# Deeper lead of logits and softmax in an attention stage, and LayerNorm rows fetched in pairs

## The chip, the cores and the metric

The kernel is one program on one core of a Trainium2 chip. The metric is device time in microseconds (us) of one execution. The core has five engines that run side by side, each through its own list of instructions and in the order of that list: TensorE (PE, matrix products), VectorE (DVE), ScalarE (ACT), GpSimd (POOL) and SyncE (SP, which here only issues DMA transfers). ACT and POOL issue DMA transfers too.

## The reference, cut to what matters

One decoder block over 1024 tokens of width 1024, in float32. A projection gives queries, keys and values, the input of a convolution, and merge gates. The attention has 8 heads in 2 groups and three branches (compressed, selected, window); the selection takes 16 of 16 blocks, so the selected branch is causal attention over all keys. Beside it a convolution of width 31 is followed by a LayerNorm over 512 channels and a product with `w_conv_out`. The two paths are gated, summed and multiplied by `w_out`; a gated feed-forward part and a gated embedding term (`p @ w_ple`) follow.

```python
o = gates[0] * o_c + gates[1] * o_s + gates[2] * o_w
y_a = o @ w_o_nsa[i]
c = jax.nn.silu(layernorm(c, conv_ln_g[i], conv_ln_b[i]))
y_b = c @ w_conv_out[i] + b_conv_out[i]
h = h + (ga * y_a + gb * y_b) @ w_out[i]
...
h = h + gate * (p[i] @ w_ple[i])
```

## The kernel before

Every product keeps float32 precision by splitting both operands into a high and a low part (ACT writes the high part, DVE or POOL subtracts it from the original) and adding three products. Weights come through `w_fetch`, which keeps two raw tiles in flight on SP's queue, and `w_split`, which splits the oldest of them (ACT L102, then L105 on DVE, or on POOL during attention); `w_get` hands out split weights in the order of one list, and splits on the spot when none is ready.

The two calls of `attention(g, ...)` are the stage that the change touches. The work of a group is 32 *units*: 8 blocks of 128 queries (`i`), 2 pairs of heads (`hp`), 2 branch kinds (`br` 1: compressed and selected keys, 2: window). A unit runs through three steps. `qk_steps` makes logits: PE multiplies queries with keys into a PSUM bank, and DVE moves them, masked and with their row maximum, into the unit's tile S in SBUF (L677, L689, L692). `soft_steps` is the softmax: DVE reduces the maximum (`ngm`, L712), ACT takes the exponent (L717), DVE makes the factor `r` (L721, L722), POOL multiplies blocks of S by it (L702, `norm`). `av_steps` makes the products with the values: PE transposes a pair of blocks of S (L758), ACT and DVE split them into P (L160, L161), and PE multiplies P by v. The last of these comes three steps late (`LAG = 3`), so that the split has time.

S has two tiles for each kind of branch:

```python
un.S = at([128, 2, T], "S1", bufs=2)
...
un.S = at([128, 2, 640], "S2", bufs=2)
```

`attention` goes over the units in order, and `weave` merges lists of steps by position: the products of unit n, the logits of unit n+2 in the first tenth, the softmax of unit n+1 in the first half, and filler steps that give PE work. A tile framework then simulates the program and fixes the order of each engine's instructions: a step that is written first has priority, but one that the simulation finds ready may be put ahead of it. On the chip that order is kept.

The filler of `attention(0)` is merge-gate chunks (`chunk_fill`, products of `u` with weights). The filler of `attention(1)` is, in this order: two gate chunks (the last one is chunk 31); `swap`, which closes the pool of `u`, opens the pool `cx` in its place and reads four tiles of 512 KB back on POOL's queue (L918); eight LayerNorm rows, of which `ln_b0` reads one from DRAM (`y_d`) on SP's queue and `ln_b1` transposes it on PE (L193) and splits it into `c2`; then `yb_fill` (y0 to y7, products of `c2` with `w_conv_out`) and `pw_fill` (p0, p1, p2, the embedding term; p3 is made elsewhere). Gate results, LayerNorm rows, and the tiles of `yb_fill` and `pw_fill` share three buffers of 4 KB per partition (tag "t").

The diff touches the list of weights (`late`), `attention`, `ln_b0`, `ln_b1` and the list `fill1`:

Of the kernel before, what the change touches and what calls it, by code (L numbers as in the profile page):

```python
# [34 lines left out]
def tile_hybrid_block(ctx: ExitStack, tc: tile.TileContext, a: dict, out: bass.AP):  # L35
    nc = tc.nc
# [26 lines left out]
    def weave(*lists):  # L63

        items = []
        for li, (l, lo, hi) in enumerate(lists):
            for j, f in enumerate(l):
                items.append((lo + (hi - lo) * (j + 0.5) / len(l), li, f))
        for _, _, f in sorted(items, key=lambda x: x[:2]):
            f()  # L70
# [17 lines left out]
    def w_fetch():  # L88
        while order and len(raws) < AHEAD:
            key, src, n, pl, th, tl = order.pop(0)  # L90
            raw = wp.tile([128, n], F32, tag="wr", name=nm("wr"))
            nc.sync.dma_start(raw, src)
            raws.append((key, raw, n, pl, th, tl))

    def w_split():

        w_fetch()
        if raws and raws[0][3] in pools:
            key, raw, n, pl, th, tl = raws.pop(0)
            hi = pools[pl].tile([128, n], F32R, tag=th, name=nm("wh"))  # L100
            lo = pools[pl].tile([128, n], F32R, tag=tl, name=nm("wl"))
            nc.scalar.activation(hi, raw, AF.Copy)  # L102
            for c0 in range(0, n, 512):
                cs = slice(c0, min(c0 + 512, n))
                lo_eng[0].tensor_tensor(lo[:, cs], raw[:, cs], hi[:, cs], op=ALU.subtract)  # L105
            raw_of[key] = raw
            made.append((key, (hi, lo)))
# [24 lines left out]
    for c in [0, 1] + gate_chunks[NDENSE:NDENSE + NFILL] + [2, 3] + gate_chunks[NDENSE + NFILL:]:  # L132
        add_z(c)
    EARLY, NE = (3,), 4
    late = ["y0", "y1", "p0", "y2", "p1", "y3", "y4", "p2", "y5", "y6", "p3", "y7"]
    late = [f for f in late if f[0] == "y" or int(f[1]) not in EARLY]
    held = None
    for f in late:
# [78 lines left out]
    y_d = dp.tile([8, 128, 512], F32, name="y_d")  # L217
# [395 lines left out]
    at = Pool("at", 6)  # L613
# [37 lines left out]
    def qk_steps(un):  # L651

        i, g = un.i, un.g
        KK = KS[g] if un.br == 1 else KW[g]
        th, t0 = i // 4, 128 * (i % 4)

        def step(h, si):
            if h == 0 and si == 0:
                un.mx = as_([128, 2, 8], "mx")
                if un.br == 1:  # L660
                    un.S = at([128, 2, T], "S1", bufs=2)
                    if un.hp == 0:
                        cbank[i] = (at([128, 4, 64], "cs", bufs=2), as_([128, 4], "cmx"))
                else:
                    un.S = at([128, 2, 640], "S2", bufs=2)
            S = un.S[:, h]
            q = Q[th][2 * g + un.hp][:, h, t0:t0 + 128]
            s, e = un.segs[si]
            ps = tt_()
            mm(ps[:, 0:e - s], q, KK[0][:, un.k0 + s:un.k0 + e], True, False)  # L670
            mm(ps[:, 0:e - s], q, KK[1][:, un.k0 + s:un.k0 + e], False, True)
            o = 0
            if un.nc and si == 0:
                o = un.nc
                C, cmx = cbank[i]
                hd = 2 * un.hp + h
                nc.vector.tensor_tensor_reduce(out=C[:, hd], in0=ps[:, 0:64], in1=cm[:, i], scale=0.125,  # L677
                                               scalar=-3e38, op0=ALU.add, op1=ALU.max,
                                               accum_out=cmx[:, hd:hd + 1])
            n = e - s - o  # L680
            d = slice(s + o - un.nc, e - un.nc)
            mxo = un.mx[:, h, si:si + 1]
            mask = None
            if si == un.nseg - 1:
                mask = dm[:, 512 - n:512]
            elif un.br == 2 and i >= 4 and si == 0:
                mask = em[:, 0:n]
            if mask is not None:
                nc.vector.tensor_tensor_reduce(out=S[:, d], in0=ps[:, o:e - s], in1=mask, scale=0.125,  # L689
                                               scalar=-3e38, op0=ALU.add, op1=ALU.max, accum_out=mxo)  # L690
            else:
                nc.vector.tensor_scalar(S[:, d], ps[:, o:e - s], 0.125, -3e38, op0=ALU.mult, op1=ALU.max,  # L692
                                        accum_out=mxo)

        return [(lambda h=h, si=si: step(h, si)) for h in range(2) for si in range(un.nseg)]
# [8 lines left out]
    def soft_steps(un):  # L704

        i, g = un.i, un.g
        nk = un.n - un.nc
        gi = un.br * 8 + g * 4 + un.hp * 2

        def s_max():  # L710
            un.ngm = as_([128, 2], "ngm")
            nc.vector.tensor_reduce(un.ngm, un.mx[:, :, 0:un.nseg], axis=AX.X, op=ALU.max, negate=True)  # L712
            un.sm = as_([128, 2], "sm")
            un.r = as_([128, 2], "r")

        def s_exp(h):
            nc.scalar.activation(un.S[:, h, 0:nk], un.S[:, h, 0:nk], AF.Exp, bias=un.ngm[:, h:h + 1],  # L717
                                 accum_out=un.sm[:, h:h + 1])

        def s_r():  # L720
            nc.vector.reciprocal(un.r, un.sm)  # L721
            nc.vector.tensor_mul(un.r, un.r, gts[:, i, gi:gi + 2])  # L722

        def c_sub():
            C, cmx = cbank[i]
            nc.gpsimd.tensor_tensor(C, C, cmx.unsqueeze(2).to_broadcast([128, 4, 64]), op=ALU.subtract)
            nc.scalar.activation(C, C, AF.Exp)

        def c_norm():
            C, cmx = cbank[i]  # L730
            csm, rc = as_([128, 4], "csm"), as_([128, 4], "rc")
            nc.vector.tensor_reduce(csm, C, axis=AX.X, op=ALU.add)
            nc.vector.reciprocal(rc, csm)
            nc.vector.tensor_mul(rc, rc, gts[:, i, g * 4:g * 4 + 4])
            nc.gpsimd.tensor_tensor(C, C, rc.unsqueeze(2).to_broadcast([128, 4, 64]), op=ALU.mult)

        st = [s_max, lambda: s_exp(0), lambda: s_exp(1), s_r]
        if un.cmp:
            st.insert(1, c_sub)
            st.insert(3, c_norm)  # L740
        st += [lambda b=b: norm(un, b) for b in range(min(NAHEAD, (un.nb + 1) // 2))]
        return st
# [79 lines left out]

    WA, WB, WC = 0.5, 3, 0.1

    def attention(g, pre, fill, tail=()):

        units = [Unit(i, g, hp, br) for i in range(8) for hp in range(2) for br in (1, 2)]
        nu = len(units)
        est = [units[n].av + (units[n + 2].qk if n + 2 < nu else 0) for n in range(nu)]
        total = sum(t for t, _ in fill)  # L830
        want = [max(WA * e, WB - e) + WC for e in est]
        scale = total / sum(want)
        weave((qk_steps(units[0]) + soft_steps(units[0]) + qk_steps(units[1]), 0, 1), (pre, 0, 1))
        due, done = 0.0, 0.0
        for n, un in enumerate(units):
            lists = [(av_steps(un), 0, 1)]
            if n + 2 < nu:
                lists.append((qk_steps(units[n + 2]), 0, 0.1))
            if n + 1 < nu:
                lists.append((soft_steps(units[n + 1]), 0, 0.5))  # L840
            due += want[n] * scale
            fl = []
            while fill and (done + 0.5 * fill[0][0] < due or n == nu - 1):
                t, f = fill.pop(0)
                done += t
                fl.append(f)
            lists.append((fl, 0, 1))
            if n >= nu - 2:
                m = len(tail) // 2
                lists.append((tail[:m] if n == nu - 2 else tail[m:], 0, 1))  # L850
            weave(*lists)
# [38 lines left out]
    pre, fill0 = q1 + [f for _, f in fill0[:8]], fill0[8:]  # L890
# [17 lines left out]
    hold = {}  # L908
# [8 lines left out]
                O[th][pr] = hold["o0"]([128, 2, 512], "o", F32R)  # L917
                nc.gpsimd.dma_start(O[th][pr].rearrange("p a t -> p (a t)"), o_d[2 * th + pr])  # L918

    def ln_b0(i):  # L920
        hold["y", i] = at([128, 512], "t", bufs=3)
        nc.sync.dma_start(hold["y", i], y_d[i])

    def ln_b1(i):
        if i % 4 == 0:
            c2[i // 4] = half_tiles(hold["cx"], "p", 2)
        tr_split(hold.pop(("y", i)), c2[i // 4], i)
        if i < 6:
            ln_b0(i + 2)
        if i in (3, 5):  # L930
            w_split()

    def yb_fill(c):
        st = {}
# [42 lines left out]

    fill1 = [f for c in gate_chunks[NDENSE + NFILL:] for f in gate_fill(c)]
    pre = [f for _, f in fill1[:10]]
    fill1 = fill1[10:] + [(0.1, swap), (0.1, lambda: (ln_b0(0), ln_b0(1)))] + [(0.45, lambda i=i: ln_b1(i)) for i in range(8)]  # L980
    for f in late:
        fill1 += yb_fill(int(f[1])) if f[0] == "y" else pw_fill(int(f[1]))
    attention(1, pre, fill1)
    while pend:
# [663 lines left out]
```

## Time and profile before

| what | value |
|---|---|
| time, median of 3 runs | 1594.17 us (1591.61 to 1594.58) |
| the profiled execution's own time | 1597.87 us |
| its span in the profile | 1596.1 us |
| PE busy | 1552.8 us, 97% of the span |
| DVE, ACT, POOL busy | 1213.9, 782.5, 358.3 us |
| mean granted clock of PE | 0.991 |

The span is what the profiler saw of the execution from its first to its last instruction; the execution's own time is 1.8 us more. The granted clock is PE's clock as a share of 2.4 GHz; its other level is 1.2 GHz, so a window at 0.50 was wholly at the lower one. The two calls of `attention` lie between about 300 and 705 us of the span.

### The profile page before, as it was taken

How to read it: one execution, taken by the hardware profiler on the slowest of the kernel's cores; microseconds unless marked ns; L12 is line 12 of the kernel's file. 1: busy time of each engine (PE TensorE's matmuls, PEld its weight loads, DVE VectorE, ACT ScalarE, POOL GpSimd, SP SyncE). 2: the span in 40 equal slices, each digit the busy share in tenths (PEclk: the TensorE clock that was granted, in tenths of full speed). 3: DMA queues.
4: the chain of work that ended last, by engine and by line, in shares of the span. 5: the costliest groups of instructions: out<-in, count | busy, mean ns of one | idle time of the engine just before them, and what ended most of it. 6: DMA issues, size and time to landing. Idle time of an engine off the chain costs nothing. (4 is left out here: it accounts for less than half of the span.)

```text
span 1596.1 us, 22098 instructions
## 1 busy us (share of the span) xinstructions
PE 1552.8 (97%) x7746; PEld 1312.3 (82%) x7746; DVE 1213.9 (76%) x2334; ACT 782.5 (49%) x1480; POOL 358.3 (22%) x380
## 2 busy tenths in 40 slices
PE   9999999999999899999898999999999999999998
PEld 8888889888988789987787888888888868877886
DVE  4999788566764677866999898898878768678654
ACT  5113324555665677742366544554445456445332
POOL 2000005555663476530010111111011200000000
PEclk9999999999999999999999999999999999999999
DMA  4223233111012623257133232322322478574421
GB/s 163 67 92 122 70 128 132 73 54 54 32 68 101 205 93 113 95 207 287 45 137 128 73 126 99 112 100 99 114 101 102 138 250 284 173 225 132 144 80 53
DMA packets 77583, 194.40 MB, mean 122 GB/s; under 512 B 8608, under 2 KB 8992, under 8 KB 77472
## 3 DMA queue, kind: packets, MB, share of 16 engines
q1 hardware_dynamic: 57312, 146.58, 26.8%
q10 hardware_dynamic: 18720, 41.16, 6.9%
q0 software_dynamic: 1440, 5.24, 1.0%
q8 instruction: 61, 1.00, 0.3%
q14 instruction: 50, 0.41, 0.1%
HBM read 140.26 MB, written 52.69 MB: 121 GB/s over the span
## 5 line engine op out<-in xcount | busy, mean ns | idle before, releaser
L164 PE MATMUL t<-T,S 128*128 128x512 f32 x1320 | 309.7, 389 | 0.2 <-ACT f L1280 0.2
L164 PEld LDWEIGHTS t<-T,S 128*128 128x128 f32 x1320 | 247.6, 188 | 52.4 <-ACT f L1280 0.7
L164 PE MATMUL t<-u,wh 128*128 128x512 f32 x1024 | 287.3, 393 | 0.4 <-DVE u L269 0.3
L164 PEld LDWEIGHTS t<-u,wh 128*128 128x128 f32 x1024 | 189.2, 189 | 37.6 <-DVE ms L247 0.6
L164 PE MATMUL t<-wh,a 128*128 128x512 f32 x616 | 192.9, 392 | 6.4 <-ACT wh L1410 6.2
L164 PE MATMUL t<-u,wl 128*128 128x512 f32 x512 | 164.8, 392 | 0.0
L102 ACT ACTIVATE wh<-wr 128x1024 fp32r<-128x1024 f32 (+2 forms) x80 | 77.0, 964 | 177.2 <-PE t L164 108.8
L702 POOL TENSOR_TENSOR S<-S,r 128x512 f32<-128x512 f32 (+1 forms) x152 | 137.8, 930 | 100.2 <-DVE r L722 54.8
L331 DVE SCALAR_TENSOR_TENSOR s<-s,cw,s 128x1019 f32<-128x1019 f32 (+16 forms) x120 | 152.0, 1271 | 2.9
L1296 POOL TENSOR_TENSOR f<-f,f 128x1024 f32<-128x1024 f32 x22 | 64.2, 2917 | 389.8 <-DVE f L1326 214.6
L164 PEld LDWEIGHTS t<-wh,a 128*128 128x128 f32 x616 | 114.9, 188 | 33.5 <-ACT wh L1410 9.3
L164 PE MATMUL t<-wl,a 128*128 128x512 f32 x308 | 120.5, 392 | 1.4 <-DVE wl L1411 1.3
L161 DVE TENSOR_TENSOR P<-t,P 128x512 fp32r<-128x512 f32 (+1 forms) x168 | 97.7, 595 | 30.3 <-ACT P L160 29.5
L160 ACT ACTIVATE P<-t 128x512 fp32r<-128x512 f32 (+1 forms) x168 | 84.3, 525 | 65.5 <-PE t L758 57.7
L164 PE MATMUL t<-T,wh 128*128 128x512 f32 x352 | 113.0, 393 | 0.4 <-ACT wh L102 0.4
L164 PE MATMUL t<-P,v 128*128 128x256 f32 x528 | 105.7, 301 | 5.3 <-DVE P L161 2.6
L164 PEld LDWEIGHTS t<-u,wl 128*128 128x128 f32 x512 | 95.3, 188 | 18.7
L717 ACT ACTIVATE S<-S,ngm 128x640 f32<-128x640 f32 (+7 forms) x128 | 93.2, 732 | 30.2 <-DVE ngm L712 29.2
L689 DVE CUSTOM_DVE_ANT_0 S<-t,mk 128x320 f32<-128x320 f32 (+9 forms) x160 | 76.3, 489 | 19.7 <-PE t L164 18.9
L105 DVE TENSOR_TENSOR wl<-wr,wh 128x512 fp32r<-128x512 f32 x101 | 66.8, 698 | 30.0 <-ACT wh L102 29.1
L1256 ACT ACTIVATE S<-s 128x512 fp32r<-128x512 f32 x88 | 54.0, 627 | 72.4 <-PE t L164 46.7
L164 PE MATMUL t<-v,v 128*128 128x512 f32 (+1 forms) x408 | 89.2, 378 | 0.0
(250 smaller groups left out, 2971.2 us busy)
## 6 DMA issues: line engine op xcount, KB each, us to landing
r<-a_d SPq DMA_DIRECT2D x77, 256.0 KB, 3.6
r<-in_w_dn_dram SPq DMA_DIRECT2D x66, 256.0 KB, 4.1
wr<-in_w_z_dram SPq DMA_DIRECT2D x32, 512.0 KB, 3.5
f<-in_w_up_dram SPq DMA_DIRECT2D x26, 512.0 KB, 3.7
wr<-in_w_up_dram SPq DMA_DIRECT2D x22, 512.0 KB, 3.3
a_d<-f ACTq DMA_DIRECT2D x44, 256.0 KB, 2.1
a_d<-s ACTq DMA_DIRECT2D x33, 256.0 KB, 2.1
s<-in_x_dram SPq DMA_DIRECT2D x8, 512.0 KB, 7.7
```

What stands on the lines that cost most here:

```text
L102: nc.scalar.activation(hi, raw, AF.Copy)
L105: lo_eng[0].tensor_tensor(lo[:, cs], raw[:, cs], hi[:, cs], op=ALU.subtract)
L160: nc.scalar.activation(hi, ps, AF.Copy)
L161: nc.vector.tensor_sub(lo, ps, hi)
L164: nc.tensor.matmul(o, l, r, start=s, stop=e, skip_group_check=True)
L331: nc.vector.scalar_tensor_tensor(ac[:, s:], c[:, :T - s], cw2[:, w0 + 30 - s:w0 + 31 - s], ac[:, s:], op0=ALU.mult, op1=ALU.add)
L689: nc.vector.tensor_tensor_reduce(out=S[:, d], in0=ps[:, o:e - s], in1=mask, scale=0.125, scalar=-3e38, op0=ALU.add, op1=ALU.max, accum_out ...
L702: nc.gpsimd.tensor_tensor(d, d, un.r.unsqueeze(2).to_broadcast([128, 2, d.shape[2]]), op=ALU.mult)
L717: nc.scalar.activation(un.S[:, h, 0:nk], un.S[:, h, 0:nk], AF.Exp, bias=un.ngm[:, h:h + 1], accum_out=un.sm[:, h:h + 1])
L1256: nc.scalar.activation(hi, src, AF.Copy)
L1296: nc.gpsimd.tensor_tensor(o, zg[j], o, op=ALU.mult)
```

## The change

Three edits. First, in `attention` the logits are made three units ahead of the products instead of two, and the softmax two units ahead instead of one (`QK, SM = 3, 2`); the start-up that comes before unit 0 grows accordingly. The number of S tiles stays. Second, `ln_b0` reads two LayerNorm rows into the halves of one tile; the first two pairs are asked for inside the last gate chunk (8 and 3 steps before its end) instead of after `swap`, and the third and fourth pair after rows 1 and 3. Third, `p0` moves from behind y1 to the front of the list of weights, its four steps are put between the LayerNorm rows, and the two calls of `w_split` in `ln_b1` go.

```diff
-    late = ["y0", "y1", "p0", "y2", "p1", "y3", "y4", "p2", "y5", "y6", "p3", "y7"]
+    late = ["p0", "y0", "y1", "y2", "p1", "y3", "y4", "p2", "y5", "y6", "p3", "y7"]
...
+    QK, SM = 3, 2
...
-        est = [units[n].av + (units[n + 2].qk if n + 2 < nu else 0) for n in range(nu)]
+        est = [units[n].av + (units[n + QK].qk if n + QK < nu else 0) for n in range(nu)]
...
-        weave((qk_steps(units[0]) + soft_steps(units[0]) + qk_steps(units[1]), 0, 1), (pre, 0, 1))
+        first = [f for n in range(SM) for f in qk_steps(units[n]) + soft_steps(units[n])]
+        weave((first + [f for n in range(SM, QK) for f in qk_steps(units[n])], 0, 1), (pre, 0, 1))
...
-            if n + 2 < nu:
-                lists.append((qk_steps(units[n + 2]), 0, 0.1))
-            if n + 1 < nu:
-                lists.append((soft_steps(units[n + 1]), 0, 0.5))
+            if n + QK < nu:
+                lists.append((qk_steps(units[n + QK]), 0, 0.1))
+            if n + SM < nu:
+                lists.append((soft_steps(units[n + SM]), 0, 0.5))
...
-    def ln_b0(i):
-        hold["y", i] = at([128, 512], "t", bufs=3)
-        nc.sync.dma_start(hold["y", i], y_d[i])
+    def ln_b0(q):
+
+        t = at([128, 2, 512], "t", bufs=3)
+        for r in range(2):
+            hold["y", 2 * q + r] = t[:, r]
+            nc.sync.dma_start(t[:, r], y_d[2 * q + r])
...
-        if i < 6:
-            ln_b0(i + 2)
-        if i in (3, 5):
-            w_split()
+        if i in (1, 3):
+            ln_b0(i // 2 + 2)
...
-    fill1 = fill1[10:] + [(0.1, swap), (0.1, lambda: (ln_b0(0), ln_b0(1)))] + [(0.45, lambda i=i: ln_b1(i)) for i in range(8)]
-    for f in late:
+    fill1 = fill1[10:]
+    fill1.insert(-8, (0.1, lambda: ln_b0(0)))
+    fill1.insert(-3, (0.1, lambda: ln_b0(1)))
+    fill1 += [(0.1, swap)]
+    ps_ = pw_fill(0)
+    lb = [(0.45, lambda i=i: ln_b1(i)) for i in range(8)]
+    fill1 += lb[:2] + ps_[:1] + lb[2:4] + ps_[1:3] + lb[4:6] + ps_[3:] + lb[6:]
+    for f in late[1:]:
         fill1 += yb_fill(int(f[1])) if f[0] == "y" else pw_fill(int(f[1]))
```

## Rows read from the trace of the kernel before

**Rows 1.** Windows of both attention calls: PE, PEld, DVE, ACT, POOL busy, clock, DMA.

```profile
340.00:380.00 40.00, 36.30 (x205) 32.34 (x206) 27.10 (x105) 23.64 (x60) 22.50 (x28) 0.87 0.08 27
...
535.00:580.00 45.00, 37.66 (x227) 33.64 (x226) 34.95 (x123) 32.38 (x83) 24.66 (x27) 0.92 0.42 150
...
sum 405.00, PE 390.92 PEld 349.03 DVE 275.40 ACT 262.21 POOL 226.04; mean PE 39.09 PEld 34.90 DVE 27.54 ACT 26.22 POOL 22.60
```

**Rows 2.** PE's waits, 300 to 712 us: total, times, longest, in us.

```profile
PE t L193 <- DMA t<-y_d: 5.4, 1, 5.4
PE t L164 <- DVE P L161: 2.6, 3, 1.2
PE t L758 <- POOL S L702: 2.3, 3, 1.5
PE t L164 <- ACT P L160: 1.8, 1, 1.8
PE t L164 <- DVE mx L689: 0.6, 1, 0.6
PE t L164 <- DVE ngm L712: 0.5, 1, 0.5
PE t L164 <- ACT t L475: 0.4, 1, 0.4
```

**Rows 3.** Windows behind the longest waits (columns: PE, PEld, DVE, ACT, POOL, clock, DMA).

```profile
341.30:347.00 5.70, 5.70 (x23) 4.93 (x23) 4.70 (x13) 3.21 (x9) 4.36 (x7) 0.70 0.00 0
373.40:380.00 6.60, 6.57 (x31) 6.23 (x32) 5.00 (x15) 3.10 (x8) 4.50 (x6) 0.58 0.00 0
541.10:545.00 3.90, 3.90 (x19) 3.81 (x20) 2.07 (x6) 1.68 (x5) 1.61 (x2) 0.50 0.75 266
545.00:549.00 4.00, 4.00 (x30) 3.97 (x30) 2.05 (x8) 3.24 (x7) 1.31 (x2) 0.85 0.40 137
```

**Rows 4.** Timeline of PE, 532 to 546 us: start, us, instruction, idle before.

```profile
533.85 1.03 PE L193 MATMUL t<-ident,t 128*128 128x128 f32 x8
534.64 1.05 PE L164 MATMUL t<-ks,q 128*128 128x448 f32 x4
541.08 1.08 PE L193 MATMUL t<-ident,t 128*128 128x128 f32 x4 [5.38 <-DMA t<-y_d]
```

**Rows 5.** SP's timeline, line L922's landing times, and DMA issues 519 to 546 us.

```profile
534.48 1.06 SPq L922 DMA_DIRECT2D t<-y_d  x2
...
DMA to landing us min/median/max: 2.6/3.2/6.5
...
o<-o_d POOLq DMA_DIRECT2D x4, 512.0 KB, 6.0
```

**Rows 6.** Timeline of ACT and POOL, 545 to 553 us: the split of p0's weights.

```profile
546.56 1.05 ACT L102 ACTIVATE wh<-wr 128x1024 fp32r<-128x1024 f32 x1
...
547.68 5.04 POOL L105 TENSOR_TENSOR wl<-wr,wh 128x512 fp32r<-128x512 f32 x4 [4.35 <-ACT wh L102]
```

**Rows 7.** Timeline of all engines, 335 to 343 us: a softmax chain and its readers.

```profile
339.14 0.15 DVE L722 TENSOR_TENSOR r<-r,gts 128x2 f32<-128x2 f32 x1
...
339.46 3.18 POOL L702 TENSOR_TENSOR S<-S,r 128x512 f32<-128x512 f32 x4 [0.63 <-DVE ngm L712]
...
339.57 0.94 DVE L722 TENSOR_TENSOR r<-r,gts 128x2 f32<-128x2 f32 x1
...
340.56 1.03 PE L758 MATMUL t<-ident,S 128*128 128x128 f32 x6 [0.65 <-POOL S L702]
```

**Rows 8.** Timeline of ACT, 372 to 373.5 us: the split that PE waited for.

```profile
371.79 0.81 ACT L717 ACTIVATE S<-S,ngm 128x640 f32<-128x640 f32 x1
...
372.72 0.60 ACT L160 ACTIVATE P<-t 128x512 fp32r<-128x512 f32 x1
```

**Rows 9.** PE's timeline, 557.7 to 561.2 us, and line L689's own durations.

```profile
558.01 0.82 PE L758 MATMUL t<-ident,S 128*128 128x128 f32 x6
...
559.26 0.43 PE L164 MATMUL t<-ks,q 128*128 128x288 f32 x2
...
L689 DVE CUSTOM_DVE_ANT_0 S<-t,mk x160: 283/488/685, 300.3 to 686.9; 128x320 f32<-128x320 f32 x64, 128x128 f32<-128x128 f32 x16, 128x256 f32<-128x256 f32 x16, 128x384 f32<-128x384 f32 x16
```

## The prediction

> **What bounds the kernel now.** I read the page first: PE is busy nearly throughout, so only what PE loses can be won, and the change removes no instruction of PE. Next come windows over the stage that the diff touches. In the 405 us from 300 to 705 us PE was busy 390.9 us; DVE, ACT and POOL were busy 275, 262 and 226 us, none of them near the whole [rows 1]. The reader is to see that no engine but PE is full, and that the lost 14 us are therefore waits of PE and not another engine's load. The view of PE's waits names them [rows 2]: seven causes, 5.4 + 2.6 + 2.3 + 1.8 + 0.6 + 0.5 + 0.4 = 13.6 us, and one of them, the LayerNorm row from DRAM, is 40% of it. Last, windows behind the long waits show a second cost: the granted clock was 0.70, 0.58, 0.50 and 0.85 there [rows 3], and the level below 2.4 GHz is 1.2 GHz. PE was busy all through, so what it lost is length times what is missing to 1.0: 5.7 x 0.30 = 1.7 us, 6.6 x 0.42 = 2.8 us, and 3.9 x 0.50 + 4.0 x 0.15 = 2.6 us. The short waits elsewhere (1.5 us and less, alone) left no such window. Ceiling: 13.6 + 1.7 + 2.8 + 2.6 = 20.7 us.
>
> **LayerNorm rows, removed wait.** PE transposed rows 0 and 1 at 533.85, had the logits of one unit behind them, was done at 535.7, and then stood until 541.08 at row 2 [rows 4]. Row 2's load was issued at 534.48, when row 0's buffer came free; it took about 6.5 us where the median row took 3.2, because four loads of 512 KB from `swap` ran beside it, each 6.0 us to landing [rows 5]. After the change rows 0 to 3 are asked for inside chunk 31, before `swap` exists, in two of the three 4 KB buffers. The third takes the gate's result, as now. So row 2 is there at 535.7: 5.4 us of idle and the 2.6 us of low clock behind it go, 8.0 us. What is late next: rows 4 and 5 now take row 2's place behind `swap`'s loads (issue at about 534.5, landing near 541). They are covered by rows 2 and 3, three steps of p0 and the attention steps woven between; I count nothing.
>
> **p0 moved into the rows.** The same instructions of PE, ACT, POOL and DMA, elsewhere. Before, the weights p and pl of p0 were split while y0 ran: ACT 1.05 us each, POOL 5.04 us in a row for the four low parts [rows 6]. Now `w_get` splits both on the spot. They live in `cx`, which lies where `u` lay, so the split cannot begin before the last gate product, which PE has behind it when it starts rows 0 and 1 at 533.85 [rows 4]. From about 533, with POOL's 5.04 us behind ACT's 1.05 us, p0's second product is ready at about 539, and later if POOL's queue serves softmax blocks first. PE is through with rows 0 and 1 and one unit's logits at 535.7. So between 0 (rows 2 and 3 and a unit's products are ordered ahead) and 3.3 us plus low clock, up to the present 8.0, comes back. The co0 raw load on SP is queued behind it as well, since p's raw tile must come free first; co0's ACT split then stands in ACT's list. The loss of the two `w_split` calls makes the weights come one step of the list ahead instead of two, and pl of p2 is split on the spot also (ACT 1.05, POOL half of the 5.04); it has attention steps as cover. For all of these I take 2.0 us, nearer to nothing, because the order on PE is made from a simulation that knows the weights are late; the DMA under load, which caused the present wait, is not part of them. LayerNorm and p0 together: 8.0 - 2.0 = 6.0 us.
>
> **Softmax two units ahead.** At 339.14 the factor r of a unit is made, at 339.46 POOL begins its blocks, and PE's transposes of these blocks start at 340.56, just when the first is done: the chain has no slack [rows 7]. One unit more of lead is about 405 us / 64 = 6.3 us. That takes away all waits of the transposes for POOL and the wait for ngm: 2.3 + 0.5 = 2.8 us [rows 2]. The waits for P (2.6 + 1.8 = 4.4 us), with 1.7 + 2.8 = 4.5 us of low clock behind them [rows 3], are mixed. In the longest, ACT reached the split only at 372.72, behind an exponent of 0.81 us that had itself waited for its maximum [rows 8]; an exponent with a unit of slack no longer stalls the list, but the same number of exponents and evictions still stands ahead of splits. Bounds 0 and 8.9 us; I take half, 4.4 us. The waits for mx and for the gate's tanh (1.0 us) have nothing to do with the lead: 0.
>
> A rule speaks against the second half. At 339.57 r took 0.94 us, and the POOL multiplication beside it ran from 339.46; alone, at 339.14, r took 0.15 us [rows 7]. The Trainium skill, "SBUF — State Buffer", section "SBUF: two separate sides", says that VectorE and GpSimd share one pair of ports under an exclusive lock, held for a whole instruction. The row agrees; by that rule the change moves no work off POOL, DVE goes on standing still with P's splits behind it, and the sum would be 4.4 us less. I keep the half and make the rest a rival.
>
> **Logits three units ahead.** No work added. But S has two tiles per branch kind, and units of one kind alternate: the logits of n+3 go into the tile of n-1, whose last transposes come directly before, where n+2 used the tile of n-2, free for a whole unit. DVE's eviction now waits for those transposes; behind it on DVE stand P's splits. In the trace the order is transposes, P products, logits (558.01, 559.26), and an eviction takes 0.49 us [rows 9]. PE's own order thus hides it: the matmul before an eviction is already behind the transposes. Bounds: 0, and one eviction in each of the 58 units that have logits ahead (29 per group), 28 us. I take 1.0 us. Start-up is longer by one unit's logits and softmax, woven with 24 and 10 filler steps where PE never waited; the shifted weights `est` redistribute the same filler. Both 0; without that filler each would cost a softmax chain, some 3 us.
>
> **Sum.** 6.0 + 2.8 + 4.4 - 1.0 = 12.2 us. The profiled execution took 1597.87 us, 3.7 us over the median of the runs; 1597.87 - 12.2 = 1585.7, and on the scale of the median 1594.17 - 12.2 = 1582.0 us.
>
> **Rivals.** *The wait changes its name* (0.18): the split of p0's weights, or the ACT list behind co0's late load, holds PE in the rows as long as row 2 did. For it: 539 against 535.7, and POOL also serving S blocks. Against: there is attention work to put ahead. All 6.0 us are lost: gain 6.2, 1588.0 us. *The lead does not reach P's splits* (0.15): DVE goes on standing still beside POOL's multiplications (0.94 against 0.15 us for r), and the 4.4 us stay: gain 7.8, 1586.4 us. (The Trainium skill states this lock as a rule, on the page named above.) *Both* (0.12): 1.8 us, 1592.4 us, no change that can be told. *The S tile* (0.15), slower: each of the 58 units holds PE until the last transposes of n-1 let DVE evict. At 0.3 us a unit that is 17.4 instead of 1.0 us: 12.2 - 16.4 = -4.2, 1598.4 us. It decides from (12.2 + 1.0) / 58 = 0.23 us a unit, half an eviction. Against it: PE's order above, and DVE is busy only 68% of the stage [rows 1].
>
> **How the numbers follow.** The forecast itself has 0.40. A measurement of this kernel tells a change from none at about 0.2%, 3.2 us: faster is below 1591.0, slower above 1597.4. Faster: nearly all of the forecast (0.39), most of the first two rivals (0.14 and 0.13), a quarter of the third (0.03): 0.69. Slower: most of the S tile's (0.12) and some of the others' tails (0.03): 0.15. The rest is 0.16. The forecast's own range is 1577 to 1587. The range goes down to the ceiling, 1594.2 - 20.7 = 1573.5, and up until only the worse part of the S tile's cases is left out, 1597.
>
> **What will show it.** Right: PE's waits no longer list y_d, nor S from POOL; the clock windows near 541 and 373 are at 1.0; the P waits are about halved. The weights' rival shows as a wait of PE for POOL's wl (L105) or p near 535 to 541. The lock's shows as P waits of 4 us and more with r at about 1 us beside POOL. The S tile's shows as idle DVE before L689 released by PE's L758, and PE waits for mx in many units. What would make it wrong: new waits made by the reordering where there were none (620 to 705 us), or a gap long enough to drop the clock again.

## The result and the profile after

The changed kernel took 1584.45 us, median of 4 runs (1583.68 to 1585.37), against 1594.38 us before (1591.61 to 1594.6). The ratio is 0.9933 with the interval [0.992, 0.9945]: 9.9 us less, where 12.2 were forecast and 1582.0 us stood as the time. The profiled execution took 1584.88 us, 13.0 less than the one before (1597.87).

The total is close to the forecast; the terms behind it are not. PE's waits from 300 to 712 us in the kernel after (total, times, longest) answer to [rows 2]:

```profile
PE t L164 <- DVE r L722: 5.8, 1, 5.8
PE t L164 <- DVE P L161: 1.3, 2, 0.8
PE t L164 <- ACT P L160: 1.1, 1, 1.1
PE t L758 <- DVE P L161: 1.1, 1, 1.1
PE t L758 <- POOL S L702: 0.3, 1, 0.3
PE t L785 <- POOL cs L735: 0.3, 1, 0.3
PE t L164 <- DVE mx L689: 0.2, 1, 0.2
```

The row from DRAM (y_d, 5.4 us) is gone from the list. A wait of 5.8 us that was not there before stands at its head. The waits for S from POOL fell from 2.3 to 0.3 us, those for ngm and the tanh are gone, and those for P fell from 4.4 to 1.3 + 1.1 + 1.1 = 3.5 us. Windows of the kernel after, over the stretches of [rows 1] and behind the new wait:

```profile
340.00:380.00 40.00, 39.71 (x252) 35.53 (x251) 31.36 (x135) 28.95 (x72) 26.04 (x34) 1.00 0.14 46
...
535.00:580.00 45.00, 44.47 (x282) 40.42 (x282) 37.76 (x139) 33.98 (x86) 29.27 (x34) 0.97 0.35 118
```

```profile
532.20:538.00 5.80, 5.80 (x25) 5.34 (x26) 2.42 (x11) 2.71 (x8) 5.68 (x7) 0.54 0.32 91
```

From 340 to 380 us PE is now busy 39.7 of 40 us at a clock of 1.00 (36.3 at 0.87 before): the loss of that stretch is gone whole. From 535 to 580 us it is busy 44.5 of 45 us (37.7 before), mostly because the wait around the rows now lies ahead of that window: 5.8 us of waiting, and behind it 5.8 us at 0.54, which is 5.8 x 0.46 = 2.7 us more. The timeline of the kernel after, all engines, shows what PE stood for:

```profile
523.90 0.60 PE L193 MATMUL t<-ident,t 128*128 128x128 f32 x4
...
524.58 0.60 PE L193 MATMUL t<-ident,t 128*128 128x128 f32 x4
...
525.21 0.96 SPq L928 DMA_DIRECT2D t<-y_d  x2
...
525.72 0.60 PE L758 MATMUL t<-ident,S 128*128 128x128 f32 x4
...
528.50 1.06 ACT L102 ACTIVATE wh<-wr 128x1024 fp32r<-128x1024 f32 x1
...
529.64 2.50 POOL L105 TENSOR_TENSOR wl<-wr,wh 128x512 fp32r<-128x512 f32 x2 [2.24 <-ACT wh L102]
529.87 0.61 ACT L717 ACTIVATE S<-S,ngm 128x384 f32<-128x384 f32 x1
...
530.46 0.60 ACT L717 ACTIVATE S<-S,ngm 128x384 f32<-128x384 f32 x1
...
531.06 1.04 ACT L102 ACTIVATE wh<-wr 128x1024 fp32r<-128x1024 f32 x1
...
532.16 0.29 PEld L164 LDWEIGHTS t<-wh,wh 128*128 128x128 f32 x1 [6.08 <-ACT wh L102]
532.16 0.79 PE L164 MATMUL t<-wh,wh 128*128 128x512 f32 x1 [5.84 <-DVE r L722]
...
535.52 1.05 PE L193 MATMUL t<-ident,t 128*128 128x128 f32 x4
```

Rows 0 and 1 are transposed at 523.9 and 524.6, ten microseconds sooner than before [rows 4]. PE has S transposes left until 526.3, and then its list says p0's first product, whose two operands are both `wh`: the high parts of p and pl. ACT hands out the first at 529.56; two exponents of the softmax stand ahead of the second, which ends at 532.10; PE starts at 532.16. The view of waits names r because r ended at 532.15, the last before PE went on; the weight load's row (`<-ACT wh L102`) names the weights, and the kernels below that split them elsewhere test that.

One place in the next stage serves as a clock mark: a product `t<-wh,s` that stands behind the same wait of 1.40 us in every kernel here. In the timelines of PE, before and after:

```profile
726.32 1.43 PE L164 MATMUL t<-o,wh 128*128 128x512 f32 x4 [2.33 <-ACT wh L102]
768.62 1.20 PE L164 MATMUL t<-wh,s 128*128 128x512 f32 x4 [1.40 <-ACT s L1048]
```

```profile
754.98 1.20 PE L164 MATMUL t<-wh,s 128*128 128x512 f32 x4 [1.40 <-ACT s L1058]
```

The changed kernel is there 13.6 us sooner, which is all of the 13.0 us between the two profiled executions. The first row of before is a wait for the weights that the o products use, 14 us behind the window that I had asked for; after, it is gone. For some kernels below I also give PE's low clock from 296 to 744 us: windows of 4 us, the busy time of PE in each times what its clock lacks to 1.0, summed. It is 8.3 us before and 2.7 after; where a window is partly idle, the sum comes out a little too small.

### The profile page after: what moved, and what is told of

It is laid out like the page before. It is cut to its first block, busy times and chain, and to the rows that moved or that the text cites. A ratio compares the mean times of both kernels' runs of the same rounds, so it can differ in the third digit from the quotient of the medians.

```text
span 1583.2 us, 22120 instructions
## 1 busy us (share of the span) xinstructions
PE 1547.4 (98%) x7746; PEld 1308.5 (83%) x7746; DVE 1215.8 (77%) x2334; ACT 781.0 (49%) x1480; POOL 358.4 (23%) x380
## 5 line engine op out<-in xcount | busy, mean ns | idle before, releaser
L102 ACT ACTIVATE wh<-wr 128x1024 fp32r<-128x1024 f32 (+2 forms) x80 | 77.0, 964 | 166.7 <-PE t L164 105.5
L1333 ACT ACTIVATE f<-f,cv 128x1024 f32<-128x1024 f32 x44 | 54.6, 1240 | 67.6 <-DVE f L1292 50.0
```

Source lines behind the costliest of these rows:

```text
L1333: nc.scalar.activation(o, z, AF.Identity, bias=cv[:, C_FB + c:C_FB + c + 1], scale=cv[:, wc + 2:wc + 3])
```

## Experiments

After the result the theory was: the LayerNorm part moved its wait on to p0's weights and won nothing, and the lead won all. The rival: each part wins by itself. The two halves first.

**The leads alone**, rows and p0 as before:

```
+    QK, SM = 3, 2
...
+        first = [f for n in range(SM) for f in qk_steps(units[n]) + soft_steps(units[n])]
...
+            if n + QK < nu:
+                lists.append((qk_steps(units[n + QK]), 0, 0.1))
+            if n + SM < nu:
+                lists.append((soft_steps(units[n + SM]), 0, 0.5))
```

> Logits three and softmax two units ahead; LayerNorm rows and p0 as before the change. Theory A (the lead wins in full, the row edits win nothing because row 2's wait of 5.4 us became a wait of 5.8 us for p0's weights): about 9 us faster, 1585.5 us; the waits of PE for S from POOL and most of those for P are gone, row 2's wait of about 5 us is there with a clock window of 0.5 behind it. Rival B (the row edits carry a good part, 4 us or more): 1589 us or more. Rival C (the S tile holds evictions): PE waits for mx, DVE idle for PE's transposes before L689, 1590 us or more.

1587.35 us, ratio 0.9958 [0.9944, 0.9973]; mark at 761.08. Its two long waits, in PE's timeline:

```profile
533.90 1.09 PE L193 MATMUL t<-ident,t 128*128 128x128 f32 x4 [8.06 <-DMA t<-y_d]
...
718.98 3.49 PE L164 MATMUL t<-o,wh 128*128 128x512 f32 x8 [2.63 <-ACT wh L102]
```

All waits of the first group's 339 to 373 us and those at 562 to 585 us are gone; the wait for row 2 grew from 5.4 to 8.1 us, since PE comes to it sooner (the wait begins at 533.90 - 8.06 = 525.8 us, where it began at 535.7 before). The time lies between theory A's 1585.5 us and rival B's 1589.

**Rows and p0 alone**, the changed kernel with the leads of before:

```
-    QK, SM = 3, 2
+    QK, SM = 2, 1
```

> Lead as before the change (two and one); LayerNorm pairs and p0 among the rows as after. Theory A: within 2 us of the kernel before, 1592.5 to 1596.5 us; no wait for a LayerNorm row, but one of 4 to 6 us for p0's weights; the softmax waits (POOL S, P) are still there. Rival B: 1588 to 1590 us.

1585.79 us, ratio 0.9954 [0.9939, 0.9969]; mark at 758.98; low clock 4.1 us. PE's timeline:

```profile
372.09 0.39 PE L164 MATMUL t<-P,v 128*128 128x256 f32 x1 [1.79 <-ACT P L160]
...
538.16 0.79 PE L164 MATMUL t<-wh,wh 128*128 128x512 f32 x1 [4.02 <-DVE p L161]
718.26 1.21 PE L164 MATMUL t<-o,wh 128*128 128x512 f32 x4 [0.93 <-ACT wh L102]
```

The theory that this half wins nothing fell: by the ratio it is worth 7.3 us, and the time lies under rival B's 1588 to 1590 us too. At the rows themselves it wins little (4.0 us for p0's weights in place of 5.4 for row 2). The rest lies elsewhere: the waits of 1.48, 0.41 and 0.51 us at 562 to 585 us are gone, the one for the o weights fell from 2.33 to 0.93. By the ratios the halves give 6.7 and 7.3 us by themselves and 10.7 together, each to within some 2.4 us, in part because both remove those 2.4 us.

**Pairs, with p0 behind y1 again** (leads as after):

```
-    late = ["p0", "y0", "y1", "y2", "p1", ...
+    late = ["y0", "y1", "p0", "y2", "p1", ...
...
+        if i in (3, 5):
+            w_split()
...
-    fill1 += lb[:2] + ps_[:1] + lb[2:4] + ps_[1:3] + lb[4:6] + ps_[3:] + lb[6:]
+    fill1 += [(0.45, lambda i=i: ln_b1(i)) for i in range(8)]
```

> The lead and the LayerNorm pairs as after the change; p0 back behind y1, with the two splits in the LayerNorm rows, as before. Theory A (p0's split on the spot is the wait of 5.8 us): neither the wait for a row nor the one for p0's weights, 8 us of idle and low clock less than the changed kernel, 1576.5 us. Rival D (the place is short of something else, such as ACT or POOL behind the rows, and any filler would wait there): a wait of 3 us or more under another name, 1582 to 1586 us.

**The splits of p0's two weights, and of the next one, placed between the rows, p0's products behind all of them:**

```
-    fill1 += lb[:2] + ps_[:1] + lb[2:4] + ps_[1:3] + lb[4:6] + ps_[3:] + lb[6:]
+    sp = [(0.1, w_split)]
+    fill1 += lb[:1] + sp + lb[1:3] + sp + lb[3:5] + sp + lb[5:] + ps_
```

> As after the change, but p0's weights and the next one are split by steps between the LayerNorm rows, and p0's four products come behind the last row. Theory A: the wait for p0's weights goes, 1576.5 to 1579 us. Rival D: a wait of 3 us or more near the rows stays, 1582 to 1586 us.

1582.24 us, ratio 0.9927 [0.9913, 0.9941], and 1582.51 us, 0.9927 [0.9911, 0.9944]; marks at 757.00 and 753.40. PE's timeline, first of the former, then of the latter:

```profile
533.75 1.07 PE L193 MATMUL t<-ident,t 128*128 128x128 f32 x4 [2.49 <-DMA t<-y_d]
...
714.76 3.64 PE L164 MATMUL t<-o,wh 128*128 128x512 f32 x8 [2.17 <-ACT wh L102]
```

```profile
533.83 1.09 PE L193 MATMUL t<-ident,t 128*128 128x128 f32 x4 [2.67 <-DMA t<-y_d]
```

In both the 5.84 us are gone, so p0's split on the spot, with its product right behind, was their cause. A wait for row 4 comes instead: p0's products no longer stand between rows 3 and 4, PE comes to row 4 at 531.2 us, and its load, requested at 525 to 528 us with `swap`'s four reads beside it, has not landed. The medians lie about 2 us under the changed kernel's, within the intervals. So theory A had the cause and not the gain; the times are those of rival D.

**Is it `swap`'s loads that make the row late?** First I put the four reads of o_d behind row 7 in the order of the program, in the kernel before and in the kernel with the splits ahead:

```
+    def o_back():
...
+    fill1 = ... [(0.45, lambda i=i: ln_b1(i)) for i in range(8)] + [(0.1, o_back)]
```

> The kernel before, with one edit: the four reads of 512 KB that the swap issues on the POOL queue come behind the eighth LayerNorm row (they are needed only by the output products, 150 us later). Theory E (row 2's load was slow because these four ran beside it): row 2's wait falls from 5.4 us to 2 us or less, and the low clock behind it goes, 5 to 8 us faster, 1586 to 1589 us. Rival F (it waits for its buffer or for the queue, and would also without them): the wait stays above 4 us, time as before within 2 us.

> The kernel of e4 (lead, pairs, p0's weights split ahead and its products behind the rows) with the same four reads behind the last row. Theory E: its wait of 2.7 us for row 4 goes with the low clock behind it (7.2 us at 0.77, 1.7 us), 4 us below e4, 1578 us. Rival F: row 4 still waits 2 us or more, 1582 us.

1598.62 us, ratio 1.0016 [1.0007, 1.0026], and 1582.19 us, 0.9919 [0.9906, 0.9932]. PE's waits for the rows stay (6.3 and 2.7 us), but neither tells anything of the question. POOL's issues in the former:

```profile
528.35 1.67 POOL L922 DMA_DIRECT2D o<-o_d  x3
532.60 0.60 POOL L922 DMA_DIRECT2D o<-o_d  x1
```

That is about where they were before (529.56): nothing that the reads need was moved, and POOL came to them early. So next the reads were tied to row 7's result: POOL copies one column of that result into each tile before the read overwrites it.

```
+                nc.gpsimd.tensor_copy(O[th][pr][:, 0, 0:1], c2[1][1][1][:, 1, 511:512])
```

> The kernel before; the four reads of 512 KB of the swap are made to wait for the eighth LayerNorm row by a copy of one column per tile on POOL (128 by 1 element each, overwritten by the read), since in e5 the order alone did not hold them back (they were issued at 528 to 533 us all the same). Theory E (they share the DMA engines with row 2's load): row 2's load lands in some 3 us, its wait falls to 2 us or less, 5 to 7 us faster. Rival F: the wait stays above 4 us.

> The kernel of e4 with the same copies, so that the reads come behind the last row. Theory E: row 4's wait of 2.7 us goes, 3 to 4 us below e4 on the same scale, ratio to the kernel before 0.990. Rival F: it stays, ratio 0.992 to 0.993.

1595.49 us, ratio 1.0001 [0.9989, 1.0012], and 1582.33 us, 0.9914 [0.99, 0.9928]. The reads now start at 552.7 and 545.6 us. DMA issues from 516 to 560 us (KB each, median us to landing), splits ahead without and then with the reads held:

```profile
o<-o_d POOLq DMA_DIRECT2D x4, 512.0 KB, 6.2
t<-y_d SPq DMA_DIRECT2D x4, 256.0 KB, 7.7
```

```profile
o<-o_d POOLq DMA_DIRECT2D x4, 512.0 KB, 9.4
t<-y_d SPq DMA_DIRECT2D x4, 256.0 KB, 3.3
```

The same four rows, asked for from the same time on (525.7 and 525.9 us), land in 3.3 instead of 7.7 us (medians), and PE no longer waits for them. In the kernel before with the reads held, PE's timeline:

```profile
536.62 0.63 PE L193 MATMUL t<-ident,t 128*128 128x128 f32 x4 [2.31 <-DMA t<-y_d]
538.71 1.94 PE L193 MATMUL t<-ident,t 128*128 128x128 f32 x8 [1.02 <-DMA t<-y_d]
```

The 5.38 us became 2.31 (row 2) + 1.02 (row 3). Row 2, requested at 533.10, lets PE go on 3.5 us later, where it took 6.5 before; so `swap`'s reads were the greater part of row 2's lateness, as the prediction had it from [rows 5]. The rest is the load's own 3 us, which only an earlier request removes. The Trainium skill, "DMA: Bandwidth & Descriptors", section "Issuing engines are not separate DMA queues", says that transfers issued from SP, ACT and GpSimd run on the same 16 DMA engines and interleave there; the 7.7 against 3.3 us agree. It buys almost nothing in time, so theory E was right about the waits and not about the time. Before: 2.1 us of waiting at the rows, in an interval of 1.8 us to either side, and the low clock in all stays at 8.2 us. The clock behind the two short waits was 0.71 from 538.7 to 549 us, so the low clock there (10.3 x 0.29 = 3.0 us) cost no less than the 2.6 us behind the one long wait; and a new wait of 2.04 us for P at 561.79 us had 7.2 us at 0.76 behind it. With the splits ahead: the mark moves from 753.40 to 752.93 only, since PE, 3 us sooner at that place, meets new waits:

```profile
562.30 0.63 PE L758 MATMUL t<-ident,S 128*128 128x128 f32 x4 [0.85 <-DVE cmx L677]
579.62 0.73 PE L164 MATMUL t<-p,wh 128*128 128x512 f32 x2 [1.59 <-DVE ngm L712]
```

**Which lead?** The changed kernel with one of the two leads set back, `QK, SM = 3, 1`, and `QK, SM = 2, 2` with the softmax steps spread from 0.1 to 0.6 of the unit:

> As after the change, but only the logits keep the longer lead (three), the softmax is one unit ahead again. Theory G (it is the softmax chain that had no slack): the waits near 339 and 370 us of 5 us together with their low clock are back, about 8 us slower than the changed kernel, 1592 us. Rival H (it is the logits' lead): they stay away, 1584.5 us. If the S tile costs something, it costs it here too: waits of PE for mx.

> As after the change, but logits and softmax both two units ahead (the softmax a tenth of a unit later in its unit, so that it comes behind its logits). Theory G: nearly all of the gain of the lead, 1584 to 1587 us. Rival H: the waits are back, 1590 us or more.

1584.46 us, ratio 0.9933 [0.9918, 0.9948], and 1588.6 us, 0.9959 [0.9945, 0.9974]. PE's timeline in the first group, of the former and of the latter:

```profile
342.56 1.01 PE L758 MATMUL t<-ident,S 128*128 128x128 f32 x6 [1.40 <-POOL S L702]
```

```profile
318.82 0.44 PE L758 MATMUL t<-ident,S 128*128 128x128 f32 x2 [1.61 <-POOL S L702]
369.65 0.66 PE L758 MATMUL t<-ident,S 128*128 128x128 f32 x4 [0.54 <-POOL S L702]
372.14 0.62 PE L164 MATMUL t<-P,v 128*128 128x256 f32 x3 [0.69 <-DVE P L161]
375.09 0.57 PE L785 MATMUL t<-ident,cs 128*128 128x128 f32 x2 [2.34 <-POOL cs L735]
```

With the same rows, the four settings of (logits, softmax) give 0.9954 for (2, 1), 0.9959 for (2, 2), 0.9933 for (3, 1) and 0.9933 for (3, 2). The waits near 372 us go with the logits' third unit whatever the softmax does, and stay, in part under other names, without it. With the logits at three, the softmax's second unit takes away the 1.40 us at 342 us and leaves 0.29 + 0.27 us at the start-up (317.7 us), a difference smaller than a measurement shows. Theory G, that it carries the gain, fell; H was right about the waits and the time of (3, 1), while 1588.6 us for (2, 2) lies between G's 1587 and H's 1590, and the intervals of (3, 1) and (2, 2) still touch. What the logits' lead relieves is the exponent on ACT, which waits for its maximum. ACT's waits of that kind from 300 to 500 us (total, times, longest) for (2, 1), (2, 2) and (3, 1):

```profile
ACT S L717 <- DVE ngm L712: 17.4, 12, 3.9
```

```profile
ACT S L717 <- DVE ngm L712: 14.6, 9, 3.6
```

```profile
ACT S L717 <- DVE ngm L712: 6.8, 8, 3.0
```

In the kernel before they are 17.3 us, in the changed kernel 7.3.

**The change again, and a weave apart** (`WC` 0.15 instead of 0.1, which spreads the same filler a little differently):

> The changed kernel as it is, beside e10 on the same chip. Both theories: ratio 0.992 to 0.9945, and the wait of 5.8 us for p0's weights in the trace as in the first profile.

> A control: the changed kernel with the constant that spreads filler evenly over the units raised from 0.1 to 0.15, which has no purpose. Theory J (the waits belong to the stages and not to one lucky order): waits of PE from 300 to 735 us within 3 us of the changed kernel's 10 us, time within 3 us. Rival K (the gain is in good part the luck of one order): more than 4 us either way.

1583.19 us, ratio 0.9928 [0.9914, 0.9942], and 1582.61 us, 0.9923 [0.9907, 0.9938]. The gain repeats, and it is no accident of one weave. The waits of PE at p0 and at the o weights in the second one:

```profile
533.02 0.79 PE L164 MATMUL t<-wh,wh 128*128 128x512 f32 x1 [5.84 <-DVE r L722]
...
716.26 2.11 PE L164 MATMUL t<-o,wh 128*128 128x512 f32 x8 [0.64 <-ACT wh L102]
```

None of the versions that take p0's wait away is told apart from the changed kernel: the best ratio, 0.9914 [0.99, 0.9928], lies beside 0.9928 [0.9914, 0.9942] of the change run on the same chip.

## Why the prediction came out near, point by point

On the scale of the profiled execution the forecast was 1585.7 us and the execution took 1584.88: the sum was short by 0.8 us there. That it came so near is luck: 6.5 us that were forecast at the rows did not come, and 4.0 us at the o weights, which nobody forecast, with 1.0 + 1.0 + 0.8 us at three small terms made up for nearly all of it. Its terms, with what the two profiles show:

- *LayerNorm rows and p0: 6.0 forecast, -0.5 measured.* Removed were 5.4 + 2.6 us, as said; in their place came 5.84 us for p0's weights and 2.7 us of low clock. The step that failed is "nearer to nothing, because the order on PE is made from a simulation that knows the weights are late". The rival "The wait changes its name" is what happened, up to the bound that the paragraph on p0 gives (8.0 us back; 8.5 came). The bound of 539 us against 535.7 was off in both numbers: PE is through at 526.3 and the product starts at 532.16. It is the leads that bring PE there sooner: with them alone its wait begins at 525.8 us, with the rows and p0 alone at 538.16 - 4.02 = 534.1. The prediction priced the rows with the arrival of the kernel before. So the -0.5 also holds what the leads added to the wait; against the leads alone (8.06 us, with about the same low clock behind) the row edits took off 2.2 us here.
- *Rows 4 and 5 behind `swap`'s loads: nothing forecast, nothing measured.* They were requested from 525.21 us on, no row took more than 7.8 us to land, and PE, with p0's steps between, comes to row 4 only at 546.07. By these numbers row 4 would be there even if PE came 8.5 us sooner, without p0's wait and its low clock. In the pairs alone and the splits ahead that cover stands behind the rows, and row 4 cost 2.5 and 2.7 us of waiting. PE's timeline after:

```profile
546.07 0.60 PE L193 MATMUL t<-ident,t 128*128 128x128 f32 x4
```

- *POOL's S and ngm: 2.8 forecast, 2.2 measured.* The waits that were there are gone; 0.29 + 0.27 us for POOL are new, both in the start-up (317.7 and 318.5 us), which had been put at 0. The kernels with either half alone show that 1.48 + 0.51 of it, in the second group, also goes with the rows moved; why a different order of filler removes them there wasn't settled.
- *Waits for P with their low clock: 4.4 forecast, 5.4 measured* (4.4 + 4.5 before; 3.5 after, with no low clock in the first group; 1.7 of it is the low clock at 341 us, which comes and goes, see below). The rival by which the lock on the shared ports keeps these waits didn't come: r still takes up to 1.22 us on DVE after (1.28 before), but the waits near 372 us went. It was the logits' lead that removed them, which the prediction had counted as a cost only. The mechanism, an exponent that no longer stalls ACT's list, holds (17.3 us of its waits before, 7.3 after); it was credited to the wrong lead.
- *The S tile: -1.0 forecast, none measured.* PE's waits for mx fell from 0.6 to 0.2 us, and in the view of DVE's waits no group of L689 is released by PE's L758. A third tile wasn't tried.
- *Not forecast: 4.0 us.* The wait for the o weights at 726.32, 2.33 us, is gone, and with it the low clock behind it (3.68 x 0.39 + 4.00 x 0.07 = 1.7 us in the windows 726.3 to 730 and 730 to 734 before). In the five kernels profiled with p0 behind y1 (before and its two variants, the leads alone, the pairs alone) it is 2.2 to 2.7 us; in the others it is at most 0.93. So it goes with p0's place. Why p0's place matters there wasn't settled; ACT's timeline before shows that the split itself stood for the raw weight from DRAM:

```profile
725.64 0.63 ACT L102 ACTIVATE wh<-wr 128x512 fp32r<-128x512 f32 x1 [3.41 <-DMA wr<-in_w_o_dram]
```

-0.5 + 2.2 + 5.4 + 0.8 (mx and tanh, forecast at 0) + 4.0 = 11.9 of the mark's 13.6 us; 1.7 us have no term. By the medians the gain is 9.9. Part of the difference is the execution itself: before's profiled one lay 3.5 us over its median, and 1.7 us of that may be the low clock at 341 us, which no other profiled execution with those waits had (below).

## What to carry to other kernels

When a stall goes, write down the next thing PE needs at that place and when it will be there, with the time at which PE now arrives; a bound worked out with the old arrival is worth little, and another edit of the same change can move that arrival (here by ten microseconds). A cost that is nothing because other work covers it comes back when that work is moved: with p0's products behind the rows, row 4 was late; with the reads held as well, PE came 3 us sooner and met two waits in the softmax. And read the trace past the end of the stage that is changed: 4.0 of the 13.6 us lay 14 us behind the window.

## What the runs showed of the hardware

The same short waits brought the low clock in one execution and not in others. At 339 to 341 us PE waited 0.99 and 0.65 us in the profile before, and the clock behind was 0.72. In the rows-alone kernel and in both variants of before with o_d moved the same waits stand to within 0.02 us, and the clock stayed at 1.00. Of the rows-alone kernel, PE's timeline and the windows:

```profile
339.56 0.63 PE L164 MATMUL t<-P,v 128*128 128x256 f32 x3 [0.99 <-DVE P L161]
340.84 1.01 PE L758 MATMUL t<-ident,S 128*128 128x128 f32 x6 [0.65 <-POOL S L702]
```

```profile
341.00:347.00 6.00, 6.00 (x32) 4.95 (x32) 5.22 (x15) 3.45 (x11) 4.95 (x8) 1.00 0.00 0
372.00:380.00 8.00, 7.68 (x46) 7.42 (x47) 6.65 (x27) 4.68 (x12) 4.89 (x8) 0.79 0.00 0
```

Behind the pair of 1.2 and 1.8 us near 372 it fell in all four (0.57, 0.79, 0.64, 0.66). A low clock seen behind a short wait in one profile is therefore no sure term of a sum; the 1.7 us counted at 341 us were not there to win in three of these four executions.
